# Half products reordered, early blocks and late transposes moved, raw weights in another pool: a two-layer hybrid block on one core

## The chip, the cores and the metric

The kernel runs on one core of one Trainium2 chip. The metric is the device time of one execution in microseconds. Engines are named as the profile names them: PE is TensorE, DVE VectorE, ACT ScalarE, POOL GpSimd, SP the engine that issues most DMAs.

## The reference

512 tokens x and 256 context tokens, both 1024 wide, go through two layers. Each layer normalises and modulates its input, mixes tokens (a gated linear recurrence, a Fourier part and a convolution, each over a share of the columns), projects, and then runs an MLP with a squared ReLU over 4096 hidden units. The second layer needs no context output.

```python
def sq_relu_mlp(h, w1, w2):
    return jnp.square(jax.nn.relu(h @ w1)) @ w2
...
    for l in range(DEPTH):
        need_ctx = l < DEPTH - 1
        ...
        hx = modulate(rmsnorm(x, g_pre_mix[l]), mx[0], mx[1])
        hc = modulate(rmsnorm(ctx, g_pre_mix[l]), mc[0], mc[1])
        out_x, out_c = token_mixers(...)
        x = x + mx[2] * rmsnorm(out_x, g_post_mix[l])
        hx = modulate(rmsnorm(x, g_pre_mlp[l]), mx[3], mx[4])
        x = x + mx[5] * rmsnorm(sq_relu_mlp(hx, w_mlp1[l], w_mlp2[l]), g_post_mlp[l])
        if need_ctx:
            ...
```

## The kernel before

Every product of fp32 values is made of three fp32r matmuls: each operand is split into a high half (`hi`, a copy in fp32r) and a low half (`lo`, the difference), and hi x hi, hi x lo and lo x hi are added up in PSUM. A weight arrives by DMA as a raw tile; ACT makes `hi` (L219), DVE makes `lo` (L220). An activation is split the same way by `split` (L230 on ACT, L233 on DVE). `weight(...)` hands out the weights in the order of one list and prepares AHEAD = 2 further ones; so the raw tiles, the DMAs on SP and the splits follow the order in which weights are asked for.

Tiles come from pools: three raw tiles of 4 KB a partition, six `hi`, five `lo`, eight `t4` (4 KB), twenty `t3`, five `c2`, and in PSUM four banks `mm` and four `aux`. A scheduler sets the order on each engine from the order of the program and the pools; each engine then runs its own list in order.

The tokens lie in six blocks of 128 in layer 0 (context first), four in layer 1. The MLP runs in eight groups g of four hidden blocks of 128 units. From group 1 on, the first product h @ w1 is made in two pairs of hidden blocks (`mlp1_pair`), each with seven half products in place of eight, after a scheme that trades a product for additions: the hidden width is split into two blocks (results g1 and g2), the depth into two halves, and the tokens into two halves of HN (384 in layer 0, 256 in layer 1) that start at TA and TB. A11, A12, A21, A22 are the quarters of the activations, s1, s2, s4 are sums of them, built once per layer and held in t3 tiles; wb1 and wb2 are weights as loaded, wt1 and wt2 sums of them that DVE builds in the raw tiles. One half product is 12 matmuls (L1114) of HN columns. Before the change their order in a pair is: X = wb1 A11, copied to x1; Z = wb1 A12, added to x1, squared into g1's first token half; X += wt1 s2, copied to x2 (L1138); Y = wt1 s1 in aux; X += wt2 A21, copied to x3 and added to Y, squared into g2's second half; X += wt2 A22, Relu to x4 and squared into g1's second half; Y += wb2 s4, added to x2, squared into g2's first half. The second token half of g1 and g2 is thus made ahead of the first half of g2.

`mlp2` is the second product: for a block of 128 tokens and half of the 1024 columns, 12 matmuls (L1045): f = 0 to 3 over the four hidden blocks, three each. gt[0], gt[1] are the results of a group's first pair, gt[2], gt[3] of its second. Two blocks are begun early: their f = 0, 1 run between the second pair's X += wt2 A21 and X += wt2 A22; then follow the pair's last products and the rest. Results are added to one t4 tile per block (L1207).

In the last group each block's sum is normalised, multiplied by a gate row G (one t4 tile per row, L385), scaled, and added to the residual, which comes back by DMA. `unit` (L402 to L404, with a POOL power at L396) normalises it for the next layer, and `prenorm_t` turns it: eight transposes (L417) in two aux banks, scale and shift by L423 on ACT for the first four and L426 on DVE for the others, then `split` into the tiles hhi and hlo. `norm_late(DEFER)` runs the transposes one block late; after the last block `norm_late(0)` runs what is left. Behind that comes the v product of the next layer (`v_mm`, L504): first all of the first half's columns for blocks 0 to 3, then the first part of the second half's depth for the same blocks, then blocks 4 and 5.

Of the kernel before, what the change touches and what calls it, by code (L numbers as in the profile page):

```python
# [22 lines left out]
DEPTH = 2  # L23
# [41 lines left out]
def build(tc, a):  # L65
# [119 lines left out]
    def prep(n):  # L185
        while st["next"] < min(n, len(stream)):
# [12 lines left out]
            if key[0] in ("wt1", "wt2"):  # L199
                r1, r2 = pairs[key[1:]]  # L200
                if key[0] == "wt1":
                    raw = r2
                    V.tensor_tensor(r2[:, 0:512], r2[:, 0:512], r1[:, 0:512], ALU.subtract)
                    V.tensor_tensor(r2[:, 512:1024], r2[:, 512:1024], r2[:, 0:512], ALU.subtract)
                else:
                    raw = r1
                    V.tensor_tensor(r1.rearrange("p (k n) -> p k n", k=2), r1.rearrange("p (k n) -> p k n", k=2),
                                    r2[:, 512:1024].unsqueeze(1).to_broadcast([128, 2, 512]), ALU.subtract)
            elif key in pre:
                raw = pre.pop(key)  # L210
            else:
                raw = rawp.tile([128, 1024], F32, tag="raw", name=nm("raw"))
                dma(raw[:, :n_].rearrange("p (k n) -> p k n", k=p), src)
                if key[0] in ("wb1", "wb2"):
                    pairs.setdefault(key[1:], []).append(raw)
                    if key[0] == "wb2":

                        r0 = 512
# [168 lines left out]


# [79 lines left out]
    def layer(l, res, nbg, first=None):  # L468
# [43 lines left out]
        if first is None:  # L512
# [527 lines left out]
        def mlp2(ps, b, gt, ws, c0=0, c1=512, fs=range(4)):  # L1040
            for f in fs:
                hi, lo = ws[f // 2]
                th, tl = gt[f]
                for n, (hp, wp) in enumerate(((th, hi), (th, lo), (tl, hi))):
                    T.matmul(ps, hp[:, 128 * b:128 * b + 128], wp[:, f % 2, c0:c1], start=f == 0 and n == 0,  # L1045
                             stop=f == 3 and n == 2)
# [76 lines left out]
        def mlp1_pair(p, g1, g2):  # L1123
# [11 lines left out]
            wb2, wt1 = weight("wb2", l, p), weight("wt1", l, p)  # L1135
            product(X, wt1, 1, summed("s2"), False)
            x2 = c2()[:, :HN]
            S.activation(x2, X[:, :HN], AF.Copy)  # L1138
            Y = aux()
            product(Y, wt1, 0, summed("s1"))  # L1140
            wt2 = weight("wt2", l, p)
# [10 lines left out]
            product(Y, wb2, 1, summed("s4"), False)  # L1152
            V.tensor_tensor(x2, Y[:, :HN], x2, ALU.add)
            squared(x2, g2, TA)

        between = []
        for g in range(NF // 4):
# [12 lines left out]
            else:  # L1170
# [18 lines left out]
            if g < NF // 4 - 1:  # L1189
                for hf in range(2):  # L1190
                    ws = ws0 if ws0 and hf == 0 else [weight("w2", l, 4 * g + 2 * hf + i) for i in range(2)]
                    for b in oblk:
                        if hf == 0 and b in early:
                            ps = early[b]
                            mlp2(ps, b, gt, ws, fs=(2, 3))
                        else:
                            ps = mm()
                            mlp2(ps, b, gt, ws)
# [10 lines left out]
            G = {v: gate_row(l, 1, v) for v in ((0,) if last else (1, 0))}  # L1209
            ws = [ws0] + [[weight("w2", l, 4 * g + 2 + i) for i in range(2)]]  # L1210
            for b in oblk:
# [7 lines left out]
                for i, (c0, c1) in enumerate(zip(cuts, cuts[1:])):  # L1219
                    h0 = 512 * (c0 // 512)  # L1220
                    if c0 == 0 and b in early:
                        ps = early[b][:, :c1 - c0]
                        mlp2(ps, b, gt, ws[0], c0 - h0, c1 - h0, (2, 3))
                    else:
                        ps = mm()[:, :c1 - c0]
                        mlp2(ps, b, gt, ws[c0 // 512], c0 - h0, c1 - h0)
# [5 lines left out]
                    V.tensor_tensor(ac_, ac_, G[1 if b < CB else 0][:, c0:c1], ALU.mult)  # L1232
# [45 lines left out]
    gens = [None] * DEPTH  # L1278
    for l in range(DEPTH):
# [15 lines left out]
        late = []  # L1295
# [5 lines left out]
        for kind, v in gens[l]:  # L1301
# [4 lines left out]
            elif kind == "normed":  # L1306
                norm_late(0)
            else:
# [5 lines left out]
                norm_late(DEFER)  # L1314
        norm_late(0)
# [127 lines left out]
```

## Time and profile before

| | us |
|---|---|
| median of 3 runs | 1565.74 |
| lowest and highest | 1563.38, 1566.36 |
| profiled execution, its time | 1560.37 |
| its span | 1558.7 |
| PE busy in the span | 1496.6 |
| DVE, ACT, POOL busy | 1092.8, 755.4, 98.4 |
| mean granted clock of PE, share of full speed | 0.994 |

Times are device times; the profile comes from one execution, and its span leaves out some 1.7 us of that execution's time. PE's share is so high that what matters is PE's idle time: a line of the list of waits names the PE instruction that waited, the instruction that released it, and the time. On the timeline a bracket gives the idle time ahead of an instruction and what ended it. The windows give the granted clock of a stretch as a share of 2.4 GHz.

### The profile page before, as it was taken

How to read it: one execution, taken by the hardware profiler on the slowest of the kernel's cores; microseconds unless marked ns; L12 is line 12 of the kernel's file. 1: busy time of each engine (PE TensorE's matmuls, PEld its weight loads, DVE VectorE, ACT ScalarE, POOL GpSimd, SP SyncE). 2: the span in 40 equal slices, each digit the busy share in tenths (PEclk: the TensorE clock that was granted, in tenths of full speed). 3: DMA queues.
4: the chain of work that ended last, by engine and by line, in shares of the span. 5: the costliest groups of instructions: out<-in, count | busy, mean ns of one | idle time of the engine just before them, and what ended most of it. 6: DMA issues, size and time to landing. Idle time of an engine off the chain costs nothing. (4 is left out here: it accounts for less than half of the span.)

```text
span 1558.7 us, 23260 instructions
## 1 busy us (share of the span) xinstructions
PE 1496.6 (96%) x8926; PEld 1305.1 (84%) x8926; DVE 1092.8 (70%) x2101; ACT 755.4 (48%) x1471; POOL 98.4 (6%) x233
## 2 busy tenths in 40 slices
PE   7899999999998999999999998999999999999997
PEld 5878888987988888797888978888888888898886
DVE  3459997845899776665756575799755876666666
ACT  4634334536655243342524475544436665554544
POOL 0002013101000000000000011011101000000000
PEclk9999999999999999999999999999999999999999
DMA  8555436514524352442623242422314233323223
GB/s 328 134 170 189 144 129 214 188 53 143 182 94 148 95 189 86 145 136 81 189 68 109 89 150 78 148 68 71 106 65 165 82 110 108 109 95 107 82 83 135
DMA packets 65582, 197.30 MB, mean 127 GB/s; under 512 B 11904, under 2 KB 14368, under 8 KB 65472
## 3 DMA queue, kind: packets, MB, share of 16 engines
q1 hardware_dynamic: 64032, 191.10, 37.4%
q0 software_dynamic: 1440, 4.72, 1.0%
q8 instruction: 70, 1.15, 0.3%
q14 instruction: 40, 0.33, 0.1%
HBM read 183.13 MB, written 12.66 MB: 126 GB/s over the span
## 5 line engine op out<-in xcount | busy, mean ns | idle before, releaser
L219 ACT ACTIVATE hi<-raw 128x1024 fp32r<-128x1024 f32 (+1 forms) x245 | 244.6, 999 | 406.5 <-PE mm L1045 148.2
L1045 PE MATMUL mm<-hi,t 128*128 128x512 f32 (+1 forms) x1296 | 411.1, 394 | 13.7 <-ACT t L230 12.7
L220 DVE TENSOR_TENSOR lo<-raw,hi 128x1024 fp32r<-128x1024 f32 (+1 forms) x245 | 280.5, 1147 | 72.3 <-ACT hi L219 36.4
L1045 PEld LDWEIGHTS mm<-hi,t 128*128 128x128 f32 x1296 | 242.8, 189 | 74.7 <-ACT t L230 18.2
L1045 PE MATMUL mm<-lo,t 128*128 128x512 f32 (+1 forms) x648 | 254.4, 393 | 0.0
L457 PE MATMUL mm<-hhi,hi 128*128 128x256 f32 (+1 forms) x576 | 168.2, 336 | 0.0
L457 PE MATMUL mm<-hlo,hi 128*128 128x256 f32 (+1 forms) x576 | 166.0, 332 | 0.0
L457 PE MATMUL mm<-hhi,lo 128*128 128x256 f32 (+1 forms) x576 | 164.9, 331 | 0.0
L1207 DVE TENSOR_TENSOR t<-mm,t 128x512 f32<-128x512 f32 x120 | 81.8, 688 | 98.6 <-PE mm L1045 98.4
L1114 PE MATMUL mm<-hhi,hi 128*128 128x384 f32 (+1 forms) x448 | 139.3, 311 | 5.6 <-ACT c L1138 5.1
L1045 PEld LDWEIGHTS mm<-lo,t 128*128 128x128 f32 x648 | 122.5, 189 | 25.8
L1114 PE MATMUL mm<-hhi,lo 128*128 128x384 f32 (+1 forms) x448 | 138.6, 309 | 2.3 <-DVE lo L220 2.3
L1114 PE MATMUL mm<-hlo,hi 128*128 128x384 f32 (+1 forms) x448 | 138.4, 309 | 0.0
L457 PEld LDWEIGHTS mm<-hhi,hi 128*128 128x128 f32 x576 | 107.1, 188 | 15.0 <-issue 2.5
L457 PEld LDWEIGHTS mm<-hhi,lo 128*128 128x128 f32 x576 | 108.3, 188 | 11.0
L457 PEld LDWEIGHTS mm<-hlo,hi 128*128 128x128 f32 x576 | 108.0, 188 | 11.0 <-issue 0.4
L672 DVE SCALAR_TENSOR_TENSOR t<-t,half,t 128x783 f32<-128x783 f32 (+1 forms) x120 | 102.2, 888 | 0.4
L1114 PE MATMUL aux<-t,hi 128*128 128x384 f32 (+1 forms) x448 | 97.8, 308 | 0.0
L1114 PEld LDWEIGHTS mm<-hhi,hi 128*128 128x128 f32 x448 | 84.4, 188 | 9.6 <-ACT c L1138 6.8
L1114 PEld LDWEIGHTS mm<-hhi,lo 128*128 128x128 f32 x448 | 84.5, 189 | 2.6 <-DVE lo L220 2.6
L233 DVE TENSOR_TENSOR t<-c,t 128x256 fp32r<-128x256 f32 (+1 forms) x132 | 62.3, 478 | 34.4 <-ACT t L230 34.0
L1114 PEld LDWEIGHTS mm<-hlo,hi 128*128 128x128 f32 x448 | 84.4, 188 | 1.1
(244 smaller groups left out, 2729.2 us busy)
## 6 DMA issues: line engine op xcount, KB each, us to landing
raw<-w SPq DMA_DIRECT2D x128, 512.0 KB, 3.6
raw<-w_at SPq DMA_DIRECT2D x48, 512.0 KB, 3.5
raw<-w_a SPq DMA_DIRECT2D x44, 512.0 KB, 4.3
raw<-w_c SPq DMA_DIRECT2D x32, 512.0 KB, 5.1
xd<-t SPq DMA_DIRECT2D x20, 512.0 KB, 3.1
raw<-w_o SPq DMA_DIRECT2D x16, 512.0 KB, 5.0
t<-xd SPq DMA_DIRECT2D x20, 256.0 KB, 5.9
t<-x SPq DMA_DIRECT2D x8, 512.0 KB, 5.1
```

The lines of the kernel that those rows point to most:

```text
L219: S.activation(hi[:, r0:n0], raw[:, r0:n0], AF.Copy)
L220: V.tensor_tensor(lo[:, r0:n0], raw[:, r0:n0], hi[:, r0:n0].bitcast(F32), ALU.subtract)
L233: V.tensor_tensor(blk_lo, src, blk_hi.bitcast(F32), ALU.subtract)
L457: T.matmul(o[:, :n], wp[:, k, :], hp[:, k, t0:t0 + n], start=k == 0 and i == 0, stop=k == KB - 1 and i == 2)
L672: V.scalar_tensor_tensor(o, u[j][:, o0 + k:o1 + k], w, o, ALU.mult, ALU.add)
L1045: T.matmul(ps, hp[:, 128 * b:128 * b + 128], wp[:, f % 2, c0:c1], start=f == 0 and n == 0, stop=f == 3 and n == 2)
L1114: T.matmul(ps[:, :HN], wp[:, K2 * j + k, :], hp, start=first and k == 0 and i == 0, stop=k == K2 - 1 and i == 2, skip_group_check=True)
L1207: V.tensor_tensor(ac_, ps, ac_, ALU.add)
```

## The change

It consists of four parts.

1. In a pair, wb2 s4 runs third, into a bank W of its own in mm, and is added to x2 by one further DVE add; then Y is added and x2 squared at once. The last product is now X += wt2 A22. The early blocks run f = 0, 1, 2 early (18 matmuls in place of 12), and blocks whose tokens lie in the second half take f in the order 0, 1, 3, 2.
2. w2's raw weights lie in t4 tiles in layer 1 and from group 3 on in layer 0.
3. The gate rows of the last group come in halves, in t3 tiles.
4. The transposes of layer 0's last two blocks wait for a point inside the next layer's v product, after the v products of blocks 0 to 3.

```diff
@@ weights
-                raw = rawp.tile([128, 1024], F32, tag="raw", name=nm("raw"))
+                free = key[0] == "w2" and (key[1] == DEPTH - 1 or key[2] >= 12)
+                raw = t4() if free else rawp.tile([128, 1024], F32, tag="raw", name=nm("raw"))
@@ gate rows
+    def gate_halves(l, g, v):
+        G = [t3()[:, :512] for _ in range(2)]
+        for i in range(2):
+            dma(G[i], gd[l][g][v][512 * i:512 * i + 512].partition_broadcast(128))
+        return G
@@ v product
                 v_mm(part[b], b, range(VKB[1][1]), ws[1])
+            yield "rest", None
             for b in late_:
@@ mlp2
-        def mlp2(ps, b, gt, ws, c0=0, c1=512, fs=range(4)):
+        def mlp2(ps, b, gt, ws, c0=0, c1=512, fs=(0, 1, 2, 3), at=(0, 3)):
@@ mlp1_pair
             squared(x1, g1, TA)
-            wb2, wt1 = weight("wb2", l, p), weight("wt1", l, p)
+            W = mm()
+            product(W, weight("wb2", l, p), 1, summed("s4"))
+            wt1 = weight("wt1", l, p)
             product(X, wt1, 1, summed("s2"), False)
             x2 = c2()[:, :HN]
             S.activation(x2, X[:, :HN], AF.Copy)
+            V.tensor_tensor(x2, W[:, :HN], x2, ALU.add)
             Y = aux()
             product(Y, wt1, 0, summed("s1"))
+            V.tensor_tensor(x2, Y[:, :HN], x2, ALU.add)
+            squared(x2, g2, TA)
             wt2 = weight("wt2", l, p)
@@
             squared(x4, g1, TB, True)
-            product(Y, wb2, 1, summed("s4"), False)
-            V.tensor_tensor(x2, Y[:, :HN], x2, ALU.add)
-            squared(x2, g2, TA)
+
+        def order(b):
+            return (0, 1, 2, 3) if 128 * b < TB else (0, 1, 3, 2)
@@ groups
-                    mlp2(early[b], b, gt, ws0, fs=(0, 1))
+                    mlp2(early[b], b, gt, ws0, fs=(0, 1, 2), at=(0, 2))
@@
-                            mlp2(ps, b, gt, ws, fs=(2, 3))
+                            mlp2(ps, b, gt, ws, fs=(3,), at=(3, 3))
@@
-                            mlp2(ps, b, gt, ws)
+                            mlp2(ps, b, gt, ws, fs=order(b))
@@ last group
-            G = {v: gate_row(l, 1, v) for v in ((0,) if last else (1, 0))}
+            G = {v: gate_halves(l, 1, v) for v in ((0,) if last else (1, 0))}
@@ layers
-            elif kind == "normed":
+            elif kind in ("normed", "rest"):
                 norm_late(0)
@@
-                norm_late(DEFER)
-        norm_late(0)
+                norm_late(2 if v[1] == NB - 1 else DEFER)
```

In the changed program the line numbers are shifted: the weight split L219 and L220 is L221 and L222, the activation split L230 and L233 is L232 and L235, the transposes L417 are L425, v_mm L504 is L512, mlp2 L1045 is L1054, the half products L1114 are L1123, the copy L1138 of X into x2 is L1149, Relu and Square L1119 and L1120 are L1128 and L1129.

Four places show how the instructions move. In the names, the part behind `<-` is the operands: the stationary one first on PE.

PE in layer 0's group 2, where the early blocks are finished. mm_1012 and mm_1013 are the early blocks 0 and 1, mm_1017 is block 2; t3_961 and t3_962 are gt[3], which x2 fills. Before:

```order
L1045 MATMUL mm_1017_5936<-hi995_5788,t3_955_5577 128x512
L1045 MATMUL mm_1017_5936<-lo996_5789,t3_955_5577 128x512
L1045 MATMUL mm_1017_5936<-hi995_5788,t3_956_5578 128x512
L1045 MATMUL mm_1017_5936<-hi995_5788,t3_957_5579 128x512
L1045 MATMUL mm_1017_5936<-lo996_5789,t3_957_5579 128x512
L1045 MATMUL mm_1017_5936<-hi995_5788,t3_958_5580 128x512
L1045 MATMUL mm_1012_5866<-hi1000_5821,t3_961_5583 128x512
L1045 MATMUL mm_1012_5866<-lo1001_5822,t3_961_5583 128x512
L1045 MATMUL mm_1013_5873<-hi1000_5821,t3_961_5583 128x512
L1045 MATMUL mm_1012_5866<-hi1000_5821,t3_962_5584 128x512
L1045 MATMUL mm_1013_5873<-lo1001_5822,t3_961_5583 128x512
L1045 MATMUL mm_1013_5873<-hi1000_5821,t3_962_5584 128x512
```

Now, where mm_989 is the second pair's X, mm_1016 and mm_1017 are the early blocks, mm_1021 is block 2, t3_963 and t3_964 are gt[3]:

```order
L1123 MATMUL mm_989_5729<-hhi_96,lo998_5791 128x384
L1123 MATMUL mm_989_5729<-hhi_96,hi997_5790 128x384
L1123 MATMUL mm_989_5729<-hlo_97,hi997_5790 128x384
L1123 MATMUL mm_989_5729<-hhi_96,lo998_5791 128x384
L1054 MATMUL mm_1016_5891<-hi1004_5846,t3_963_5587 128x512
L1054 MATMUL mm_1016_5891<-lo1005_5847,t3_963_5587 128x512
L1054 MATMUL mm_1016_5891<-hi1004_5846,t3_964_5588 128x512
L1054 MATMUL mm_1017_5901<-hi1004_5846,t3_963_5587 128x512
L1054 MATMUL mm_1017_5901<-lo1005_5847,t3_963_5587 128x512
L1054 MATMUL mm_1017_5901<-hi1004_5846,t3_964_5588 128x512
L1054 MATMUL mm_1021_5944<-hi999_5807,t3_957_5581 128x512
L1054 MATMUL mm_1021_5944<-lo1000_5808,t3_957_5581 128x512
```

Before, f = 2 of the early blocks and f = 0, 1 of block 2 stand ahead of the first use of gt[3]'s first token half, with s4 ahead of them; now the product ahead is X += wt2 A22, and gt[3]'s first half has been made well before.

ACT in layer 0's group 3, second pair. c2_1062 is x1, c2_1072 is x2, c2_1077 is x3, c2_1088 is x4. Before:

```order
L1138 ACTIVATE c2_1072_6310<-mm_1061_6212 128x384
L230 ACTIVATE t3_1037_6092<-c2_1062_6225 128x384
L219 ACTIVATE hi1080_6358<-raw1082_6360 128x1024
L1144 ACTIVATE c2_1077_6343<-mm_1061_6212 128x384
L219 ACTIVATE hi1083_6364<-raw1085_6366 128x1024
L1119 ACTIVATE c2_1077_6343<-c2_1077_6343 128x384
L1120 ACTIVATE c2_1077_6343<-c2_1077_6343 128x384
L230 ACTIVATE t3_1039_6094<-c2_1077_6343 128x384
L1150 ACTIVATE c2_1088_6396<-mm_1061_6212 128x384
L1120 ACTIVATE c2_1088_6396<-c2_1088_6396 128x384
L230 ACTIVATE t3_1037_6092<-c2_1088_6396 128x384
L1119 ACTIVATE c2_1072_6310<-c2_1072_6310 128x384
```

Now, where c2_1078 is x2, c2_1083 is x3, c2_1094 is x4:

```order
L221 ACTIVATE hi1080_6354<-t4_1082_6356 128x1024
L1149 ACTIVATE c2_1078_6333<-mm_1066_6239 128x384
L1128 ACTIVATE c2_1078_6333<-c2_1078_6333 128x384
L1129 ACTIVATE c2_1078_6333<-c2_1078_6333 128x384
L232 ACTIVATE t3_1043_6102<-c2_1078_6333 128x384
L1158 ACTIVATE c2_1083_6372<-mm_1066_6239 128x384
L221 ACTIVATE hi1086_6387<-t4_1088_6389 128x1024
L1128 ACTIVATE c2_1083_6372<-c2_1083_6372 128x384
L1129 ACTIVATE c2_1083_6372<-c2_1083_6372 128x384
L232 ACTIVATE t3_1043_6102<-c2_1083_6372 128x384
L1164 ACTIVATE c2_1094_6431<-mm_1066_6239 128x384
L221 ACTIVATE hi1089_6393<-t4_1091_6395 128x1024
```

x2's Relu came behind x4's copy; now its whole chain follows its copy at once. The w2 copies hi1080, hi1086 and hi1089 come from t4 tiles, and hi1080 stands ahead of x2's copy.

SP at the same place. w_2 are w2's raw weights, w_1 those of the next pair, w_at the condition product's. Before:

```order
L213 DMA raw1071_6294<-w_2 128x1024
L213 DMA raw1076_6327<-w_2 128x1024
L338 DMA raw1078_6350<-w_at 128x1024
L338 DMA raw1079_6354<-w_at 128x1024
L213 DMA raw1082_6360<-w_2 128x1024
L213 DMA raw1085_6366<-w_2 128x1024
```

Now:

```order
L340 DMA raw1084_6379<-w_at 128x1024
L340 DMA raw1085_6383<-w_at 128x1024
L340 DMA raw1095_6436<-w_at 128x1024
L215 DMA t4_1082_6356<-w_2 128x1024
L340 DMA raw1096_6440<-w_at 128x1024
L215 DMA raw1103_6510<-w_1 128x1024
L215 DMA raw1106_6516<-w_1 128x1024
L215 DMA t4_1088_6389<-w_2 128x1024
L215 DMA raw1131_6671<-w_1 128x1024
L215 DMA t4_1091_6395<-w_2 128x1024
```

The four w2 loads of a group stood in two couples among the w_at loads; now three of group 3's four stand apart from each other, in t4 tiles, with loads of w_at and w_1 between them.

PE in the step between the layers. hhi and hlo are the normalised input; t4_1497 is block 5 before; mm_1525 the second half's product of block 3. Before:

```order
L504 MATMUL mm_1525_9023<-hi1389_8424,hlo_97 128x264
L504 MATMUL mm_1525_9023<-hi1513_8921,hhi_96 128x264
L504 MATMUL mm_1525_9023<-lo1514_8922,hhi_96 128x264
L417 MATMUL aux_1504_8887<-ident_sb_117,t4_1497_8856 128x128 x4
L417 MATMUL aux_1506_8899<-ident_sb_117,t4_1497_8856 128x128 x4
L504 MATMUL mm_1525_9023<-hi1513_8921,hlo_97 128x264
L504 MATMUL mm_1525_9023<-hi1513_8921,hhi_96 128x264
L504 MATMUL mm_1525_9023<-lo1514_8922,hhi_96 128x264
```

Now, where t4_1494 and t4_1513 are blocks 4 and 5, mm_1534 to mm_1537 the second half's products of blocks 0 to 3, and aux_1546 is block 4's first:

```order
L512 MATMUL mm_1537_9092<-lo1528_8918,hhi_96 128x264
L512 MATMUL mm_1537_9092<-hi1527_8917,hlo_97 128x264
L425 MATMUL aux_1538_9111<-ident_sb_117,t4_1494_8807 128x128 x4
L425 MATMUL aux_1540_9123<-ident_sb_117,t4_1494_8807 128x128 x4
L425 MATMUL aux_1542_9135<-ident_sb_117,t4_1513_8888 128x128 x4
L425 MATMUL aux_1544_9147<-ident_sb_117,t4_1513_8888 128x128 x4
L512 MATMUL mm_1534_9035<-hi1548_9215,hhi_96 128x264
L512 MATMUL mm_1535_9054<-hi1548_9215,hhi_96 128x264
L512 MATMUL mm_1536_9073<-hi1548_9215,hhi_96 128x264
L512 MATMUL mm_1537_9092<-hi1548_9215,hhi_96 128x264
L512 MATMUL aux_1546_9159<-hi1402_8456,hhi_96 128x264
L512 MATMUL aux_1546_9159<-lo1403_8457,hhi_96 128x264
```

The transposes left the middle of the v product of blocks 0 to 3 and stand at its end, four matmuls ahead of the first that reads block 4.

## Rows read from the trace of the kernel before

**Rows 1.** The page, engines: busy us, share of the span, instructions.

```profile
PE 1496.6 (96%) x8926; PEld 1305.1 (84%) x8926; DVE 1092.8 (70%) x2101; ACT 755.4 (48%) x1471; POOL 98.4 (6%) x233
```

**Rows 2.** Waits of PE (total us, times, longest) in 430:530, 540:900, 900:962, 1230:1560.

```profile
PE mm L1114 <- DVE lo L220: 2.6, 2, 2.3
PE mm L1114 <- ACT c L1138: 1.5, 1, 1.5
...
PE mm L1045 <- ACT t L230: 8.6, 4, 2.7
PE mm L1114 <- ACT c L1138: 3.6, 3, 2.3
...
PE aux L417 <- ACT t L404: 6.9, 4, 2.7
...
PE mm L1045 <- ACT t L230: 4.1, 6, 1.5
PE mm L1114 <- ACT c L1144: 0.4, 1, 0.4
```

**Rows 3.** Timeline, PE, layer 0: start, us, line, operands, count, [idle before <- releaser].

```profile
563.43 0.45 PE L1114 MATMUL mm<-hhi,hi 128*128 128x384 f32 x1 [2.27 <-ACT c L1138]
...
565.45 0.34 PE L1114 MATMUL mm<-hhi,lo 128*128 128x384 f32 x1
...
644.18 0.80 PE L1045 MATMUL mm<-hi,t 128*128 128x512 f32 x1 [2.54 <-ACT t L230]
...
709.64 0.50 PE L1045 MATMUL mm<-hi,t 128*128 128x512 f32 x1 [1.88 <-ACT t L230]
709.98 0.40 PE L1045 MATMUL mm<-lo,t 128*128 128x512 f32 x1
710.21 0.39 PE L1045 MATMUL mm<-hi,t 128*128 128x512 f32 x1
```

**Rows 4.** Windows: busy PE, PEld, DVE, ACT, POOL; granted clock, DMA share, GB/s.

```profile
430.00:497.00 67.00, 62.94 (x324) 55.78 (x323) 65.02 (x141) 35.33 (x64) 0.00 (x0) 1.00 0.32 105
643.00:648.00 5.00, 3.82 (x11) 3.07 (x12) 2.59 (x6) 1.04 (x2) 0.00 (x0) 0.66 0.22 74
953.00:958.00 5.00, 4.10 (x22) 4.11 (x23) 2.78 (x9) 4.92 (x16) 0.04 (x2) 0.66 0.36 111
```

**Rows 5.** Timeline, ACT, layer 0, groups 2 and 3.

```profile
561.53 1.06 ACT L219 ACTIVATE hi<-raw 128x1024 fp32r<-128x1024 f32 x1 [0.82 <-DMA raw<-w]
...
643.08 0.63 ACT L219 ACTIVATE hi<-raw 128x512 fp32r<-128x512 f32 x1 [0.87 <-DMA raw<-w]
643.62 0.51 ACT L230 ACTIVATE t<-c 128x384 fp32r<-128x384 f32 x1
```

**Rows 6.** Timeline, DVE: layer 0, group 2, and the step between the layers.

```profile
560.33 1.23 DVE L220 TENSOR_TENSOR lo<-raw,hi 128x1024 fp32r<-128x1024 f32 x1 [0.39 <-ACT hi L219]
...
566.67 0.55 DVE L1145 TENSOR_TENSOR c<-aux,c 128x384 f32<-128x384 f32 x1
...
942.60 0.70 DVE L220 TENSOR_TENSOR lo<-raw,hi 128x528 fp32r<-128x528 f32 x1
...
956.92 0.69 DVE L233 TENSOR_TENSOR hlo<-c,hhi 128x512 fp32r<-128x512 f32 x1
```

**Rows 7.** The page, DMA issues: KB each, median us from issue to landing.

```profile
raw<-w SPq DMA_DIRECT2D x128, 512.0 KB, 3.6
```

**Rows 8.** Timeline, PE, step between the layers.

```profile
944.94 1.09 PE L417 MATMUL aux<-ident_sb,t 128*128 128x128 f32 x8 [2.68 <-ACT t L404]
...
953.90 1.61 PE L417 MATMUL aux<-ident_sb,t 128*128 128x128 f32 x8 [2.68 <-ACT t L404]
```

**Rows 9.** Timeline, POOL, step between the layers.

```profile
937.60 0.55 POOL L396 TENSOR_TENSOR fr<-fs1m,nhalf 128x1 f32<-128x1 f32 x1 [3.75 <-ACT fs1m L391]
...
950.02 2.64 POOL L396 TENSOR_TENSOR pr<-prm,nhalf 128x1 f32<-128x1 f32 x1 [3.48 <-ACT prm L391]
```

More of the change, by code (lines that the diff above doesn't have):

```diff
@@ L1044, in mlp2 @@
                 for n, (hp, wp) in enumerate(((th, hi), (th, lo), (tl, hi))):
-                    T.matmul(ps, hp[:, 128 * b:128 * b + 128], wp[:, f % 2, c0:c1], start=f == 0 and n == 0,
-                             stop=f == 3 and n == 2)
+                    T.matmul(ps, hp[:, 128 * b:128 * b + 128], wp[:, f % 2, c0:c1], start=f == fs[0] and at[0] == 0 and n == 0,
+                             stop=f == fs[-1] and at[1] == 3 and n == 2)
         HN = 256 if last else 384
@@ L1221, in layer @@
                     if c0 == 0 and b in early:
-                        ps = early[b][:, :c1 - c0]
-                        mlp2(ps, b, gt, ws[0], c0 - h0, c1 - h0, (2, 3))
+                        ps = early[b]
+                        mlp2(ps, b, gt, ws[0], fs=(3,), at=(3, 3))
                     else:
                         ps = mm()[:, :c1 - c0]
-                        mlp2(ps, b, gt, ws[c0 // 512], c0 - h0, c1 - h0)
+                        mlp2(ps, b, gt, ws[c0 // 512], c0 - h0, c1 - h0, order(b))
                     ac_ = o[:, c0:c1]
@@ L1231, in layer @@
                     ms = ms_of(ss, f"fs{i}", ms)
-                    V.tensor_tensor(ac_, ac_, G[1 if b < CB else 0][:, c0:c1], ALU.mult)
+                    V.tensor_tensor(ac_, ac_, G[1 if b < CB else 0][c0 // 512][:, c0 - h0:c1 - h0], ALU.mult)
                 r = rstd_of(ms, "fr")
@@ L1278, in build @@
     gens = [None] * DEPTH
+    late = []
     for l in range(DEPTH):
@@ L1294, in build @@
             gens[0] = layer(0, res[0], 0, first)
-        late = []
         def norm_late(keep):
```

## The prediction, on record before the changed kernel ran

> **What bounds the kernel now.** I read the engines' busy time first [rows 1]: TensorE works for 1496.6 of 1558.7 us, so the end moves only with TensorE's work or with its 62 idle us. The change adds no matmul and takes none away; only idle time can change. Next I read who made TensorE wait, stretch by stretch [rows 2]. In groups 2 to 7 of layer 0's MLP it is 8.6 us in 4 waits for L230, the ScalarE copy that makes the fp32r half of a squared activation, and 3.6 us in 3 for L1138, the copy of X into x2; in group 1 there are 2.6 us for weights' low halves and 1.5 for L1138; in the step between the layers 6.9 us in 4 transposes' waits for L404, the scaling of a normalised block; in layer 1's MLP 4.1 us in 6 for L230 and 0.4 more. These are the places that the change edits.
>
> A wait costs more than its length. After one, the first matmul starts 0.34 us before the second, where 0.23 is usual (709.64, 709.98, 710.21 in [rows 3]), and its predecessor must run out first; estimated from these rows, 0.28 us each. And twice the clock fell after a wait, in 643 to 648 and in 953 to 958, to a mean of 0.66 of 2.4 GHz [rows 4]: 0.34 x 5 = 1.7 us in each, a part of it while idle. I charge 1.3 and 1.5.
>
> **Part 1: half products and early blocks.** Before, the last product of a pair is s4 (aux). Behind it stand an add, Relu, Square, the copy L230 and the L233 subtraction, some 2.6 us of chain at the 0.5 of 643.62 [rows 5] and the 0.55 of 566.67 [rows 6], and TensorE has only 12 matmuls of 0.23 (2.8 us) before it needs the result. Where ScalarE's queue holds something else, that is too little: at 643.08 a weight's copy that had waited 0.87 us for its transfer stood ahead of the L230 that TensorE waited for until 644.18 [rows 3, 5]. After, s4 runs third, and the last product is X(A22), which needs no add. Ahead of the first reader of x4 stand 6 matmuls of the early blocks, 12 of block 2 and 9 of block 3, because blocks 3 to 5 take f=2 last: 27 x 0.23 = 6.2 us. I take the L230 waits of layer 0 to go whole: 8.6 us, 4 restarts 1.1, clock 1.3: 11.0.
>
> L1138 copies X to x2, and the next product into X waits for it. Between x1's add and that copy TensorE had the s2 product alone; the s4 product gives ScalarE 12 matmuls more. From 563.43 to 565.45 eleven start, 0.17 each after the restart [rows 3], so this is 2.1 us. The third wait, 2.27 in group 2, came from a transfer: a weight's copy that had waited 0.82 us for it started at 561.53, ahead of L1138 in the queue [rows 5]; group 2 keeps its raw pool, so I leave it. The other two, 1.3 together, go, with restarts 1.9.
>
> Cost: 28 VectorE adds, one per pair: at most 28 x 0.55 = 15 us of VectorE [rows 6], covered by its 30% of idle time [rows 1], except in group 1, where it works 65.02 of 67 us [rows 4]. There the two adds may cost 1.1 us, while the 1.5 us wait for L1138 may go: I set group 1 at zero; its ends are 1.1 lost, and 4.1 [rows 2] with 0.8 of restarts gained.
>
> **Part 2: w2's raw weights in 4 KB tiles.** In layer 0 six of the eight tiles are sums and one is the condition row, so groups 3 to 6 pass their four w2 weights through one tile. A link is subtraction, transfer, ScalarE copy: 1.2 at 560.33 [rows 6], 3.6 [rows 7], 1.06 [rows 5], some 6 us. Followed through the order of group 3 with these durations, the second link's ScalarE copy (hi<-t4) ends 0.4 us before the copy of X can start, and the product that waits for that copy comes 1.5 us after it; the third and fourth links come 2 to 3 us before TensorE needs what stands behind them. Nearest row for a miss: the 0.82 and 0.87 that such copies waited [rows 5]. Bounds: nothing, or 1.5 us in each of four groups. I take 0.5 each, 2.0, nearer to nothing since the order leaves slack. The Trainium skill's page Perfetto Trace Analysis (Tensor Engine Instruction) speaks against this part: it holds ScalarE's and VectorE's queues to be strictly first in, first out. Both rows agree, for what was ready behind the copies did not pass them; were it otherwise, the tile would cost nothing and the sum would be 2.0 more, and by the rule in its strictest form, with no slack left, it is the slower rival below. What the raw pool gains hides no wait that is left, so it is worth nothing here.
>
> Layer 1 has four free tiles. Its six L230 waits (4.1) and the 0.4 go, with seven restarts 2.0: 6.5, less 0.5 for what such a queue may hold: 6.0.
>
> Layer 0 by this: 11.0 + 1.9 - 2.0 = 10.9.
>
> **Part 3: gate rows in halves.** Same bytes, three DMA issues more on SP. By the order of layer 0 they wait for s4's tiles, which the last pair now reads third; from there to the first use TensorE has 48 matmuls of the half products (8.3 us) and 21 of the second product (4.9), 13 us, against 3.6 for the same bytes of a weight [rows 7]. Zero.
>
> **Part 4: the layer step.** Two of the four transposes' waits, 2.68 each [rows 8], go, for the transposes of blocks 4 and 5 now follow all first v products: 5.4 + 0.6 of restarts + the 1.5 of clock = 7.5. The POOL power behind the second of them took 2.64 us, against 0.55 at 937.60 [rows 9],. I expect it to stay slow, since the change does nothing to it, but off TensorE's path.
>
> What is late next? First, the third v weight's lo, which ended at 943.30 [rows 6] while TensorE was free from 942.26 (944.94 less 2.68): 1.1 + 0.3 = 1.4 us that the transposes' wait hid. Second, block 4's own chain: behind its transposes TensorE has only block 5's, and four matmuls, before it reads block 4's halves. At 953.90 the transposes of block 5 began and at 956.92, 3.0 later, the first subtraction of its low halves, 0.69 long [rows 6, 8]; some 0.4 less at full clock makes 3.3. TensorE arrives after 16 transposes (1.7, twice the 0.85 from 944.94 to the next start) and 0.5: 1.2 late, 0.3 restart. Third, up to 0.5 for block 4's second half. Sum 3.4, so part 4 gives 4.1. Its ends: 0 (block 5's work queued ahead of block 4's on ScalarE), 7.5 (nothing new).
>
> **Sum.** 10.9 + 6.0 + 4.1 = 21.0 of 1560.4, the profiled execution's time (span 1558.7). The median of the runs shown is 5.4 above that execution; I take the same saving from it: 1565.7 - 21.0 = **1544.7 us**. About 0.2% (3.1 us) is what a measurement of this kernel tells from no change.
>
> **Rivals.**
> *More goes* (0.15): group 1's 4.9, group 2's 2.3 with 0.3, and the 2.0 that I charged for the tile: 21.0 + 9.5 = 30.5, 1535. For it: s4's 2.1 us also stand in groups 1 and 2. Against: group 1 is bound by VectorE [rows 4].
>
> *Half comes back* (0.14): the one tile costs 1.5 in each of groups 3 to 6 and the layer step gives 0: 21.0 - 4.0 - 4.1 = 12.9, 1553. For it: ScalarE's waits for transfers [rows 5].
>
> *Waits only move* (0.05): ScalarE stays late, now before X(A21) and X(A22) in place of the second product; the L230 waits come back as waits for the copies of X, 15 of the 17 us of both MLPs. That leaves 6, or less with a poorer layer step: 1559 to 1566, and the change does not do what it says. Against: 6.2 us of matmuls over a chain of 2.6.
>
> *Slower* (0.05): the single tile decides. If the link into the second w2 weight starts more than 2 us later than I find, its copy stands at the head of ScalarE's queue with the copy of X behind it and TensorE behind that, and a whole transfer shows: 3.6 + 1.06 + 1.2 + 0.3 = 6.2, with 1.5 of clock as after the waits of [rows 4]: 7.7 in each of four groups, 31, in place of 2.0: 21.0 + 2.0 - 31 = -8, so 1574. For it: 561.53 and 643.08, where such a copy did stand and wait. Against: the slack of 0.4 to 3 us in the order.
>
> **Chances and range.** Forecast case 0.61 (1538 to 1551), the others as above. Faster by over 0.2%: 0.61 + 0.15 + 0.14 = 0.90; within: the moving waits, 0.05; slower: 0.05. Range 1533 to 1557: it takes in the first two rivals, with a tile or a layer step somewhat better or worse than they have, and leaves out the last two.
>
> **What would show it.** Right: no L230 wait of the second product in either MLP but for tenths; waits for the copies of X of at most 1 us in groups 3 to 6; the two 2.68 waits gone, and two or three of 0.3 to 1.5 at the v product (now L512) for lo or for block 4's halves; no granted clock near 0.66 after the second product's start. Wrong: ScalarE copies of w2 that wait 2 us or more for DMA in groups 3 to 6, with TensorE waiting for the copy of X (now L1149); group 1 longer by over 1 us; transposes of blocks 4 and 5 waiting as before.

## The result, and the profile after

The changed kernel takes 1539.78 us (median of 4 runs, 1537.73 to 1540.9) where the kernel before, run beside it, takes 1565.99 (1563.38 to 1566.36): a ratio of 0.9835 with an interval of 0.9818 to 0.9852, 26 us less with a bound of some 3 either way. Run again on another chip (E5) it was 1539.06 against 1563.72, 0.9842 (0.9828 to 0.9855). Forecast were 1544.7 and a saving of 21.0.

The engines, from the page of the changed kernel:

```profile
PE 1493.7 (97%) x8926; PEld 1307.4 (85%) x8926; DVE 1100.4 (71%) x2129; ACT 752.6 (49%) x1471; POOL 94.9 (6%) x233
```

The span went from 1558.7 to 1539.2 us, and PE's idle time from 62 to 45.5. Who made PE wait, in the stretches of [rows 2] (430 to 530, 540 to 900, 900 to 962, and from 1230 on: the end of group 0 and most of group 1 in layer 0, groups 2 to 7, the step, layer 1):

```profile
PE mm L1123 <- DVE lo L222: 1.5, 1, 1.5
PE mm L1123 <- ACT c L1149: 0.6, 1, 0.6
...
PE mm L1123 <- ACT c L1149: 3.2, 4, 1.6
PE mm L1054 <- DVE t L235: 0.2, 1, 0.2
...
PE aux L425 <- ACT t L412: 1.8, 3, 1.1
PE mm L512 <- DVE lo L222: 1.3, 1, 1.3
PE aux L512 <- ACT hhi L232: 0.7, 1, 0.7
PE aux L512 <- DVE hlo L235: 0.2, 1, 0.2
...
PE mm L1123 <- ACT c L1149: 0.2, 1, 0.2
```

The 8.6 us and 4.1 us for the squared activations' copy are gone from the second product, but for 0.2. In groups 2 to 7 there are still 3.2 us for the copy of X into x2 (L1149), one wait each in groups 3 to 6; in the step the 6.9 us for L412 have become 1.8, with 2.2 for lo and block 4's halves beside them.

The two profiled executions differ by 19.5 us of span, the medians by 26.2. Cut by stages on PE's timeline (from the first half product of a group to that of the next, and from group 7's to the first v product of layer 1) the reason is seen:

| stage, us | before | changed | difference | forecast |
|---|---|---|---|---|
| up to group 1 (code not changed) | 467.7 | 473.2 | +5.5 | 0 |
| layer 0, group 1 | 70.3 | 66.0 | -4.3 | 0 |
| group 2 | 66.9 | 62.9 | -4.1 | -1.8 |
| groups 3, 4, 5, 6 | 67.3, 65.1, 67.1, 63.1 | 63.3, 64.6, 64.7, 63.2 | -4.0, -0.5, -2.4, +0.1 | -9.1 together |
| group 7 | 67.5 | 67.3 | -0.3 | 0 |
| v product of layer 1 up to its MLP's group 1 | 314.1 | 311.3 | -2.9 | -4.1 |
| layer 1, group 1 to the end | 309.5 | 302.8 | -6.7 | -6.0 |

The first row is put down to chance: TensorE runs the same instructions in the same order there, and the twelve other profiles have 467.5 to 471.2, so that 467.7 is a usual value and 473.2 the longest of all. As a whole the profiled execution of before was 5.6 us quicker than the median of its runs, and that of the changed kernel 1.1 slower than its own; in which stage the 5.6 lie isn't shown. Without the first row the changed stages gave 25.0 us, near the 26 of the runs. So the mechanism was right and the sum 4 us short. That it was no more than 4 is in part luck, for the stages differ from the forecast in both directions: 4.3 and 2.3 us more in groups 1 and 2 and 1.0 more in group 7 and layer 1, against 2.3 less in groups 3 to 6 and 1.2 less in the step. The experiments say why.

### The profile page after: what moved, and what is told of

Its sections match the earlier page's. It is cut to its first block, busy times and chain, and to the rows that moved or that the text cites. A ratio compares the mean times of both kernels' runs of the same rounds, so it can differ in the third digit from the quotient of the medians.

```text
span 1539.2 us, 23308 instructions
## 1 busy us (share of the span) xinstructions
PE 1493.7 (97%) x8926; PEld 1307.4 (85%) x8926; DVE 1100.4 (71%) x2129; ACT 752.6 (49%) x1471; POOL 94.9 (6%) x233
## 5 line engine op out<-in xcount | busy, mean ns | idle before, releaser
L1054 PE MATMUL mm<-hi,t 128*128 128x512 f32 (+1 forms) x1296 | 406.4, 391 | 0.2 <-DVE t L235 0.2
L221 ACT ACTIVATE hi<-raw 128x1024 fp32r<-128x1024 f32 (+1 forms) x193 | 189.7, 984 | 370.2 <-PE mm L1054 148.2
L1054 PEld LDWEIGHTS mm<-hi,t 128*128 128x128 f32 x1296 | 242.2, 188 | 55.6 <-DVE t L235 1.2
L222 DVE TENSOR_TENSOR lo<-raw,hi 128x1024 fp32r<-128x1024 f32 (+1 forms) x193 | 217.2, 1128 | 69.4 <-ACT hi L221 18.5
L1054 PE MATMUL mm<-lo,t 128*128 128x512 f32 (+1 forms) x648 | 253.7, 392 | 0.0
L1054 PEld LDWEIGHTS mm<-lo,t 128*128 128x128 f32 x648 | 121.8, 188 | 25.9
L1123 PE MATMUL mm<-hhi,hi 128*128 128x384 f32 (+1 forms) x448 | 139.3, 311 | 4.1 <-ACT c L1149 4.0
L1123 PE MATMUL mm<-hhi,lo 128*128 128x384 f32 (+1 forms) x448 | 138.5, 309 | 1.5 <-DVE lo L222 1.5
L1123 PE MATMUL mm<-hlo,hi 128*128 128x384 f32 (+1 forms) x448 | 138.4, 309 | 0.0
L1123 PE MATMUL mm<-t,hi 128*128 128x384 f32 (+1 forms) x448 | 97.4, 308 | 0.0
L1123 PEld LDWEIGHTS mm<-hhi,hi 128*128 128x128 f32 x448 | 84.4, 188 | 7.8 <-ACT c L1149 6.0
L1123 PEld LDWEIGHTS mm<-hhi,lo 128*128 128x128 f32 x448 | 84.3, 188 | 1.9 <-DVE lo L222 1.8
L1123 PEld LDWEIGHTS mm<-hlo,hi 128*128 128x128 f32 x448 | 84.4, 188 | 1.2
L235 DVE TENSOR_TENSOR t<-c,t 128x256 fp32r<-128x256 f32 (+1 forms) x132 | 62.1, 476 | 23.9 <-ACT t L232 23.4
```

Of the source, the lines that this page charges most:

```text
L221: S.activation(hi[:, r0:n0], raw[:, r0:n0], AF.Copy)
L222: V.tensor_tensor(lo[:, r0:n0], raw[:, r0:n0], hi[:, r0:n0].bitcast(F32), ALU.subtract)
L235: V.tensor_tensor(blk_lo, src, blk_hi.bitcast(F32), ALU.subtract)
L1123: T.matmul(ps[:, :HN], wp[:, K2 * j + k, :], hp, start=first and k == 0 and i == 0, stop=k == K2 - 1 and i == 2, skip_group_check=True)
```

## The experiments

Each is the changed kernel or the kernel before with one edit. E1 to E4 ran on one chip (before: 1561.18 us), E5 to E8 on one (1563.72), E9 to E12 on one (1564.36). Medians of different chips are compared by their ratio to before.

| run | median, us | ratio to before (interval) |
|---|---|---|
| E1, w2 of layer 0 in the raw pool | 1532.30 | 0.9815 (0.9797 to 0.9834) |
| E2, part 1 alone | 1535.87 | 0.9834 (0.9815 to 0.9853) |
| E3, part 4 alone | 1560.73 | 0.9995 (0.9978 to 1.0011) |
| E4, early 12, f in order | 1537.82 | 0.9850 (0.9831 to 0.9869) |
| E5, the changed kernel | 1539.06 | 0.9842 (0.9828 to 0.9855) |
| E6, E1 without part 4 | 1532.03 | 0.9797 (0.9783 to 0.9810) |
| E7, all w2 in the raw pool | 1533.96 | 0.9809 (0.9794 to 0.9825) |
| E8, E1, group 1 without background | 1535.46 | 0.9820 (0.9807 to 0.9834) |
| E9, E1 without part 3 | 1536.44 | 0.9811 (0.9789 to 0.9832) |
| E10, E1 again | 1533.24 | 0.9794 (0.9772 to 0.9816) |
| E11, E6 again | 1534.06 | 0.9799 (0.9779 to 0.9819) |
| E12, E6, group 1's steps spread | 1535.05 | 0.9802 (0.9775 to 0.9829) |

### E1 and E10: the single 4 KB tile

Where the waits for L1149 come from is seen on the changed kernel's timelines in group 5. SP issues the w2 load:

```profile
749.76 0.33 SPq L215 DMA_DIRECT2D t<-w  x1
```

The tile had just come free, with VectorE's subtraction for the w2 weight before it, which ends at 749.69:

```profile
748.47 1.22 DVE L222 TENSOR_TENSOR lo<-t,hi 128x1024 fp32r<-128x1024 f32 x1
```

ACT waits for it with everything behind it, the copy of X among it:

```profile
752.39 0.53 ACT L232 ACTIVATE t<-c 128x384 fp32r<-128x384 f32 x1
755.41 1.06 ACT L221 ACTIVATE hi<-t 128x1024 fp32r<-128x1024 f32 x1 [2.50 <-DMA t<-w]
756.37 0.47 ACT L1149 ACTIVATE c<-mm 128x384 f32<-128x384 f32 x1
```

and PE waits for that copy:

```profile
756.90 0.44 PE L1123 MATMUL mm<-hhi,hi 128*128 128x384 f32 x1 [1.64 <-ACT c L1149]
```

The transfer into the one free tile was issued at 749.76 and let ACT go at 755.41, 5.6 us later, where 3.6 is the median of such loads [rows 7]; X was complete by then, for PE had already made the next product, into Y, and stood idle from 755.26 (756.90 less 1.64). So E1 put w2's raw weights of layer 0 back:

```diff
-                free = key[0] == "w2" and (key[1] == DEPTH - 1 or key[2] >= 12)
+                free = key[0] == "w2" and key[1] == DEPTH - 1
```

> The changed kernel, but w2's raw weights of layer 0's groups 3 to 6 come from the raw pool again (layer 1 keeps the 4 KB tiles). Theory A, the single free 4 KB tile costs what is left of waits: in the changed kernel TensorE waits 3.3 us for the copy of X (L1149) in groups 3, 4, 5 and 7, each behind a ScalarE copy of w2 that waits 1.05 to 2.5 us for its DMA; with the raw pool these go, as in group 2, and the time falls by 3 to 4.5 us against the changed kernel, to about 1536. Rival B, the waits come from the traffic of the transfers, whatever the pool: L1149 waits stay at 2 to 4 us in groups 3 to 5 and the time is within 1.5 us of the changed kernel. Rival C, the raw pool is what the w2 tile relieves: wb and w_at loads come late, weight waits (lo L222) of over 1 us appear at the start of groups, and the time rises by 3 us or more.

The fourth of these waits, 0.2 us at 820.18, lies in group 6 and not in 7. In E1 PE has no wait left between 540 and 890. Groups 2 to 6 take 63.0, 62.7, 62.7, 62.7, 62.7 us, groups 1 to 7 together 447.2 where the changed kernel's two profiles have 451.9 and 450.8: 3.6 to 4.7 us. Theory A held, and the order on ACT shows how:

```profile
746.12 0.53 ACT L232 ACTIVATE t<-c 128x384 fp32r<-128x384 f32 x1
747.12 0.49 ACT L1149 ACTIVATE c<-mm 128x384 f32<-128x384 f32 x1 [0.47 <-PE mm L1123]
750.50 1.06 ACT L221 ACTIVATE hi<-raw 128x1024 fp32r<-128x1024 f32 x1 [2.89 <-DMA raw<-w]
```

The w2 copy waits 2.89 us here, longer than any copy from the one tile in the changed kernel (at most 2.77, at 816.07), but behind the copy of X and not ahead of it: with the raw pool the load is issued where nothing that PE needs stands behind it. E10 is the same kernel again.

> E1's kernel again, for comparison on one chip with the next two. All theories: ratio to the kernel before 0.980 to 0.982.

The groups came out the same (447.2 us for groups 1 to 7). The ratio, 0.9794, is a little under the 0.980 to 0.982 that was expected, which its interval takes in. By medians E6 and E7, which also have the raw pool, lie 7 and 5 us under the changed kernel on one chip (E5), and none of their runs reaches the quickest of E5. What goes beyond those 4 us shows in no stage that was edited: the part up to group 1, where nothing of the change runs, took 473.2 and 471.2 us in the changed kernel's two profiles and 467.5 to 470.2 in all others, E4 with the tile among them (468.1). Whether that is chance stays open.

### E2: the order alone

All of parts 2, 3 and 4 undone; part 1 as in the changed kernel.

```diff
-                free = key[0] == "w2" and (key[1] == DEPTH - 1 or key[2] >= 12)
+                free = False
@@
-            G = {v: gate_halves(l, 1, v) ...
+            G = {v: gate_row(l, 1, v) ...
@@
-            yield "rest", None
```

> Part 1 alone: half products reordered, early blocks of 18 matmuls and the order of f, all else as before the change. Theory A, the order is what gains in both MLPs: L230's waits of L1045 all go (12.7 us), group 1 and 2 gain as in the changed kernel, and layer 0's tile costs nothing here; only the layer step's 3 us are missing: 1566 less 23 to 26, about 1541, equal to the changed kernel within 2 us. Rival B, the 4 KB tiles carry a part of it in layer 1: waits of 0.2 to 1.5 us for L230 or L1149 stay there in most groups, and the time is 1545 or more.

1535.87 us, no wait of the second product for L232, and in all of layer 1's MLP one wait:

```profile
PE mm L1122 <- ACT c L1148: 1.4, 1, 1.4
```

Part 1 alone gives what the whole change gives, or more (0.9834 on its chip). Layer 1 from group 1 on takes 304.2 us, 5.3 of the 6.7 us less than before. The tiles of layer 1 add about 1, all in its first group: 43.7 us here and 42.4 to 43.0 wherever the tiles are. The step has a wait of 3.69 us here; the section on E9 comes back to it.

### E7: layer 1 without its tiles

E1 with `free = False`.

> The changed kernel with all w2 raw weights in the raw pool, layer 1's too (parts 1, 3 and 4 stand). Theory A, the order makes layer 1's gain, not the tiles: layer 1's groups keep 42.1 us each but for the first (43.7 as with part 1 alone), time 0.5 to 1.5 us above E1's kernel. Rival B: the tiles carry it, waits of 0.3 us or more in most groups of layer 1, 3 us or more above E1's kernel.

Theory A again: 43.7 us for layer 1's first group, 42.1 for each other one, 303.95 from group 1 to the end where E1 has 303.2; no wait in the groups but 1.3 us in the first.

### E4: early blocks and the order of f

```diff
-                    mlp2(early[b], b, gt, ws0, fs=(0, 1, 2), at=(0, 2))
+                    mlp2(early[b], b, gt, ws0, fs=(0, 1), at=(0, 1))
@@
-                            mlp2(ps, b, gt, ws, fs=(3,), at=(3, 3))
+                            mlp2(ps, b, gt, ws, fs=(2, 3), at=(3, 3))
@@
-                            mlp2(ps, b, gt, ws, fs=order(b))
+                            mlp2(ps, b, gt, ws, fs=(0, 1, 2, 3))
```

> The changed kernel, but the early blocks run f = 0, 1 only (12 matmuls early) and every block takes f = 0, 1, 2, 3. Theory A, s4's new place is what counts: behind X(A22) there are still 12 matmuls (f = 2, 3 of the two early blocks) and 12 of block 2 before block 3 wants x4, 5.6 us over a chain of 2.6; but f = 2 of the early blocks needs only the first token half. No new wait for L232 over 0.3 us, time within 1.5 us of the changed kernel. Rival B, the early matmuls cover the copy of X ahead of X(A22): with 12 in place of 18 TensorE comes there 1.4 us sooner in each of seven groups and two layers, waits for L1158 appear, 0.3 to 1.4 each, and the time rises by 4 us or more.

Between the two. No wait of the second product for L232 came, and layer 1 takes 302.7 us, as in the changed kernel. Layer 0's groups take 454.2, 2.3 to 3.4 more, with waits of 1.33 and 0.73 for the copy ahead of X(A22) (L1158) in groups 2 and 6. So s4's place is what counts; the 18 early matmuls and the order of f together are worth 2 or 3 us in layer 0, and by the medians of two chips (0.9850 and 0.9842) that can't be told from nothing.

### E8 and E12: group 1

E8 is E1 without background steps in group 1, with one call more in groups 3 to 6.

```diff
+                def step_on(g=g):
+                    if last or g != 1:
+                        background()
@@
-                background()
+                step_on()
...
+                if not last and g in (3, 4, 5, 6):
+                    background()
```

> E1's kernel with the background steps (VectorE's condition product, two each) left out of layer 0's group 1 and made in groups 3 to 6, one call more in each. Theory A, group 1 is bound by VectorE: its waits (0.6 for the copy of X, 1.5 for lo, 0.25) go, its 66.1 us fall to 63 to 64, groups 3 to 6 stay at 62.7 to 63, time 2 to 3 us below E1's kernel. Rival B, the weights of group 1 come late for another reason (raw pool, transfers): the lo wait stays over 1 us and the time is within 1 us of E1's kernel. Rival C: the added steps delay weights in groups 3 to 6 and the time rises.

Windows of E8: group 1, and a stretch in group 4.

```profile
467.00:531.00 64.00, 63.83 (x318) 57.00 (x317) 41.40 (x57) 29.16 (x47) 0.00 (x0) 1.00 0.23 74
693.00:698.00 5.00, 3.79 (x10) 3.05 (x11) 3.83 (x11) 2.18 (x4) 0.00 (x0) 0.50 0.76 263
```

Group 1 fell from 66.1 to 63.2 us, with VectorE at 41.40 of 64: the first half of theory A held. By itself E8 doesn't tell VectorE's work from the raw tiles and loads of those steps, which went with it. E1's trace does, for the longest wait. The high half of the weight that TensorE waits for was made by 487.68, and its low half was begun only at 496.25, while VectorE worked without a gap, for the most part on background steps (the third busy time of the window is VectorE's, 9.00 of 9):

```profile
486.63 1.05 ACT L221 ACTIVATE hi<-raw 128x1024 fp32r<-128x1024 f32 x1
496.25 1.22 DVE L222 TENSOR_TENSOR lo<-raw,hi 128x1024 fp32r<-128x1024 f32 x1
497.52 0.44 PE L1123 MATMUL mm<-hhi,lo 128*128 128x384 f32 x1 [1.54 <-DVE lo L222]
```

```profile
487.00:496.00 9.00, 8.40 (x47) 7.77 (x45) 9.00 (x28) 4.18 (x8) 0.00 (x0) 1.00 0.51 165
```

So it is VectorE's list that holds group 1 up. But the steps moved a small transpose that waits for their last product:

```profile
694.21 0.37 PE L365 MATMUL aux<-ident_sb,gp 128*8 128x128 f32 x1 [3.38 <-DVE gp L362]
```

3.38 us, and a clock of 0.50 around it (1.2 GHz, the lower of its two levels): group 4 took 69.4 us, and all was lost. E12 spread the steps otherwise, on E6's kernel.

```diff
+                def step_on(n, g=g):
+                    if last or g != 1:
+                        background()
+                    if not last and g in ((), (2, 3, 5), (3,), ())[n]:
+                        background()
```

> E6's kernel with group 1's background steps made in the middle of groups 2, 3 and 5, two steps more in each of four places, so that the small transpose they end in falls inside group 4. Theory A: group 1 falls from 66.1 or 66.8 to 63.2 us as in E8, the 3.4 us wait of E8's group 4 for gp does not come, groups 2 to 6 stay under 63.2: 2 to 3.5 us below E6's kernel, ratio 0.978. Rival B: the wait for gp or waits for weights in groups 2, 3 or 5 take it back, within 1 us of E6's kernel or above.

Rival B: group 1 takes 63.0 us, but groups 2 to 6 take 64.6, 64.3, 63.6, 63.2 and 64.8, with waits for the copies of X again, and 450.7 for groups 1 to 7 is more than E6's 447.6. VectorE's steps only changed places.

### E3, E6 and E11: the late transposes

E3 is the kernel before with part 4 alone.

```diff
+            yield "rest", None
@@
-            elif kind == "normed":
+            elif kind in ("normed", "rest"):
@@
-                norm_late(DEFER)
-        norm_late(0)
+                norm_late(2 if v[1] == NB - 1 else DEFER)
```

> Part 4 alone, late transposes of blocks 4 and 5, on the kernel before the change. Theory A: the two waits of 2.68 us go and lo (about 1.3), block 4's halves (about 0.9) take their place, as in the changed kernel; 3 to 4 us gained, about 1562.5. Rival B: without the order of part 1 the last group of layer 0 ends otherwise and the new waits take all: within 1 us of before. The MLP waits for L230 stay as they were (12 us over both layers).

PE's waits in groups 2 to 7 and in the step:

```profile
PE mm L1046 <- ACT t L230: 8.3, 4, 2.7
PE mm L1115 <- ACT c L1139: 3.5, 3, 2.5
...
PE aux L417 <- ACT t L404: 1.6, 2, 0.9
PE mm L504 <- DVE t L510: 1.1, 1, 1.1
PE aux L504 <- ACT hhi L230: 0.7, 1, 0.7
PE mm L504 <- DVE lo L220: 0.6, 1, 0.6
PE aux L504 <- DVE hlo L233: 0.2, 1, 0.2
```

The MLP waits stayed, the two of 2.68 went, and 2.6 us of others came. By the stage that is 3.0 us less than before (311.2), as theory A had it; 0.9995 with its interval reaches from 3.4 less to 1.7 more and decides nothing. E6 takes part 4 out where parts 1 and 3 stand.

```diff
-            yield "rest", None
@@
-            elif kind in ("normed", "rest"):
+            elif kind == "normed":
@@
-                norm_late(2 if v[1] == NB - 1 else DEFER)
+                norm_late(DEFER)
+        norm_late(0)
```

> E1's kernel (raw pool in layer 0) with part 4 undone: the transposes of blocks 4 and 5 inside the v product of blocks 0 to 3 again. Theory A, part 4 gains where part 1 stands: waits of L425 for L412 of 2 to 4 us come back in the step, lo and block 4's waits (2.1 us) go, and the time is 1.5 to 3 us above E1's kernel. Rival B, part 4 gains nothing, as its run alone left it open (ratio 0.9995 with 0.9978 to 1.0011): within 1 us of E1's kernel.

> E6's kernel again, beside E1's on one chip. Theory A, part 4 gains nothing where parts 1 and 3 stand: within 1 us of E1's kernel, on either side. Rival B, it gains: 1.5 us or more above E1's kernel. Rival C, it costs: 1.5 us or more below.

On one chip E10, with part 4, took 1533.24 us, and E11, without it, 1534.06. Waits in 890 to 962 with part 4 (E10):

```profile
PE aux L425 <- ACT t L412: 1.8, 3, 1.1
PE mm L512 <- DVE lo L222: 1.3, 1, 1.3
PE aux L512 <- ACT hhi L232: 0.7, 1, 0.7
PE aux L512 <- DVE hlo L235: 0.2, 1, 0.2
```

and without (E11):

```profile
PE aux L425 <- ACT t L412: 3.6, 4, 1.8
```

4.0 us against 3.6, and the stage from the v product to layer 1's MLP takes 310.6 and 311.5 with part 4 (E1, E10), 310.2 and 311.0 without (E6, E11). Here it gains nothing: rival B of E6, theory A of E11. Over all profiles this stage takes 309.7 to 311.5 us with part 3, part 4 or both, and without either 314.1 (before) and 312.2 (E2); so the two together are worth some 1 to 4 us, and which of them does it makes no difference that shows.

### E9: the gate rows' halves

E1 with the gate rows whole, in t4 tiles.

```diff
-            G = {v: gate_halves(l, 1, v) for v in ((0,) if last else (1, 0))}
+            G = {v: gate_row(l, 1, v) for v in ((0,) if last else (1, 0))}
```

> E1's kernel with part 3 undone: gate rows whole, in t4 tiles. Theory A, it is the halves that keep POOL's power short: with them no power in the step takes over 0.87 us, without them one takes 2.1 to 3.3 us beside two-tensor VectorE work; here the slow power returns, part 4 keeps most of it off TensorE's path, the last group of layer 0 is 0.6 longer, and the time is 0.5 to 2 us above E1's kernel. Rival B, part 3 is worth nothing, as predicted: powers stay at 0.87 or less and the time is within 0.5 us.

POOL's power for block 4 in E9, and VectorE beside it:

```profile
923.68 3.30 POOL L404 TENSOR_TENSOR pr<-prm,nhalf 128x1 f32<-128x1 f32 x1 [3.15 <-ACT prm L399]
```

```profile
923.77 1.29 DVE L1247 TENSOR_TENSOR t<-t,t 128x512 f32<-128x512 f32 x2
924.97 1.60 DVE L222 TENSOR_TENSOR lo<-raw,hi 128x528 fp32r<-128x528 f32 x2
```

The power started at 923.68 and ended at 926.98, 0.4 us behind the last of four VectorE operations with two SBUF operands each that came one upon the other. In E10, with halves, the same power:

```profile
924.09 0.85 POOL L404 TENSOR_TENSOR pr<-prm,nhalf 128x1 f32<-128x1 f32 x1 [3.48 <-ACT prm L399]
```

```profile
923.84 1.35 DVE L235 TENSOR_TENSOR hlo<-c,hhi 128x512 fp32r<-128x512 f32 x2
```

With halves VectorE's order in the step is another, and the power takes 0.85 us; the longest for a block's scale (pr) is 0.85 or 0.86 in E1, E6, E10 and E11, and 3.30 in E9, 3.31 in E2, 2.12 in E3. Theory A held for the power. In E2, which has neither part 3 nor part 4, the slow power (925.13 to 928.44) is followed by TensorE's longest wait of the step, where E6 and E11, with the halves, have 1.76 and 1.81:

```profile
929.67 1.35 PE L425 MATMUL aux<-ident_sb,t 128*128 128x128 f32 x8 [3.69 <-ACT t L412]
```

Group 7 takes 67.9 us in E9 and 67.2 with halves, and E9's median lies 3.2 us above E10's on one chip, somewhat more than the 0.5 to 2 of the theory; the intervals of the two overlap.

The Trainium skill's page SBUF — State Buffer (SBUF: two separate sides) says that a two-input VectorE operation and a GpSimd one that reads SBUF exclude each other for a whole instruction, whichever starts first. E9's rows agree that the power ends only behind the four, but they put its start 0.09 us ahead of the first. E10's agree less well: there two such VectorE operations run from 923.84 to 925.19 and the power comes through by 924.94. So that the halves make the power short is shown, and that the lock is the reason isn't: why one lot shuts it out and the other doesn't, these runs don't show.

## Why the prediction was right, and where its steps were off

- **L230's waits go** (11.0 in layer 0, 4.1 and restarts in layer 1). Right: 8.6 became 0.2 (0.4 in E5) and 4.1 nothing, and E2 shows that part 1 does it alone, E4 that s4's new place does it without the 18 early matmuls and the order of f.
- **Group 1 at zero.** Wrong by 4.3 us. I took VectorE's 65.02 of 67 us [rows 4] for a bound that no order could move. That window, 430 to 497, is for the most part the end of group 0; group 1 runs from 467.7 to 538.0, and VectorE works for 59.19 of the 71 us from 467 to 538. Nor had I counted that the clock fell there too, in 496 to 501, to 0.66:

```profile
467.00:538.00 71.00, 65.93 (x316) 57.95 (x316) 59.19 (x117) 29.54 (x47) 0.00 (x0) 0.98 0.39 126
496.00:501.00 5.00, 5.00 (x18) 4.46 (x19) 4.00 (x7) 3.10 (x7) 0.00 (x0) 0.66 0.82 269
```

VectorE's list does hold the group up (E8: 63.2 us without the background steps), but a busy engine is not one whose order can't be bettered: with two more adds to do, the waits fell from 5.1 us to 2.1 (1.5 for lo where 2.3 and 0.3 were, 0.6 for the copy of X where 1.5 was, none for an add of the second product where 1.0 was), and no fall of the clock followed.
- **Group 2's 2.27, "I leave it".** Wrong: it went. s4's 2.1 us of matmuls stand ahead of that copy there as everywhere; in the changed kernel w2's copies still wait for their transfers, 1.18 and 0.39 us, and are done before the copy of X. I had named both numbers and not set one against the other.
- **The single tile, 2.0.** The mechanism was right, the size too small: 3.2 us of waits in four places, 4.3 with their restarts at 0.28, and E1 gained 3.6 to 4.7 by taking it away. Without the tile groups 3 to 6 gain 11.7 us (E1), where the forecast without its 2.0 for the tile is 11.1 for them. The link was followed with the median transfer of 3.6; beside other loads it took 5.6 in group 5, which just spends the slack of 0.4 and 1.5. TensorE waited 1.6 us beyond that. The subtraction that freed the tile began at 748.47, 6.9 us after the copy from it had ended, so the link was stretched ahead of the transfer too; how much of the 1.6 that made isn't shown. The slower rival needed 6.2 in each group, so its sign was out of reach, but what it rests on, a waiting copy at the head of ACT's queue, is what happened: at 756.37 the copy of X followed the w2 copy that had waited until 755.41. The Trainium skill's page Perfetto Trace Analysis (Tensor Engine Instruction) has ACT's queue strictly in order, and these two rows agree.
- **Part 3, "Zero", and the power that I expected "to stay slow".** Wrong. With the halves VectorE's order is another, and the power takes 0.85 us in place of 3.3 (E9). The 2.68 waits of before had two cures in the change: neither comes back with part 4 alone (E3) nor with part 3 and not part 4 (E6, E11), where 1.8 and, in E6, 0.9 are left.
- **Part 4, 4.1.** The stage gave 2.9, and the items were near: lo 1.3 for 1.1, block 4's halves 0.9 for 1.2. But the gain is not part 4's: with part 3 in place it is nothing (E10, E11). What it removes there is 1.8 us (E11) or 2.7 (E6) of waits for blocks 4 and 5, and 2.1 or 2.2 for lo and block 4's halves come in.
- **Layer 1, 6.0.** 6.7, of which the order alone gives 5.3 (E2) and the four free tiles about 1.
- **The saving of one execution taken from the median.** The execution of before that I costed was 5.6 us quicker than the median of its runs. Where isn't shown; other executions of the same MLP hold clock falls that this one didn't have (below).

The best version of these runs is E1, the change without layer 0's tile (1532.3 and 1533.2 us, ratios of 0.9815 and 0.9794); E6 and E11, which leave out part 4 as well, can't be told from it (0.9797 and 0.9799). On one chip with the changed kernel, E7, which differs from E1 by layer 1's tiles alone, was 5.1 us quicker than it.

## What to carry to other kernels

Where a chain of small operations ends just before the engine that bounds the kernel needs it, put the product with the longest tail early and one with a short tail last; part 1, which does that, was by itself worth all of this change (E2). A further pool with a single free tile turns prefetches into a chain of transfers: here one tile cost 3.6 to 4.7 us, four gained about 1, and two or three weren't run. What counts is which ready instruction stands behind the waiting one in an engine's list. When two edits aim at one stall, take each out in turn: the one that was meant to cure it may add nothing.

## What the runs showed of the hardware that was not expected

The same wait is not always followed by a fall of the clock. In the profile of before, TensorE's clock fell after the wait of 2.54 at 644.18 [rows 3, 4], and not after that of 2.67 at 777.67. In E3, whose MLP is the same program, these stretches of group 1, 3 and 5 have:

```profile
516.00:521.00 5.00, 3.71 (x9) 3.00 (x10) 4.16 (x9) 0.63 (x1) 0.00 (x0) 0.66 0.58 184
646.00:651.00 5.00, 3.49 (x9) 2.83 (x10) 2.55 (x5) 1.04 (x2) 0.00 (x0) 0.66 0.24 86
779.00:784.00 5.00, 3.57 (x9) 2.85 (x10) 2.69 (x5) 1.04 (x2) 0.00 (x0) 0.66 0.27 97
```

A mean of 0.66 of 2.4 GHz in all three, after waits of 2.10, 2.71 and 2.33 us. Group 5 took 67.8 us in E3 and 67.1 in the profile of before, though its wait was 0.3 shorter in E3: one execution so loses some 1.1 us, by this estimate, where another doesn't, which may be a part of the spread of the kernel before, 1555 to 1567 us over 17 runs of one chip; E1, which has no wait over 1.6 us in the MLP, stayed within 1532.0 to 1533.3 there.
